# Down projection of a SwiGLU block: seven block products with stationary tokens, output by tokens

## The chip, the cores and the metric

The kernel runs on one core of one Trainium2 chip. The metric is the device time of one execution in microseconds (us). A profiled execution also leaves a trace: every instruction of the engines with its start and end, and the DMA transfers. In the trace PE is TensorE (matmul), DVE is VectorE, ACT is ScalarE, POOL is GpSimd, SP is the engine from whose queue the DMAs are issued.

## The reference

One layer of a residual block over 512 tokens with 2048 features: a mixing half (recurrent heads and attention heads), then a feed-forward half. Only the end of it is touched here:

```python
mod = silu(c) @ w_ada + b_ada                    # six rows of 2048: sh1, sc1, gt1, sh2, sc2, gt2
...
h2 = modulate(rms_norm(x, g_ffn), sh2, sc2)
gate, up = split(h2 @ w_up, 2)                   # w_up: 2048 x 11264, each half 5632 wide
x = x + gt2 * ((silu(gate) * up) @ w_down)       # w_down: 5632 x 2048, x: 512 x 2048
```

Everything is float32. Inside the kernel each factor of a large product is split into two parts that TensorE takes in its fp32r format, hi and lo, and a product is three matmuls: hi·hi, hi·lo, lo·hi.

## The kernel before

The kernel is traced by a planner: it records instructions in program order, finds the dependences, and orders each engine's instructions by a priority (program order, moved earlier by `tc.high_priority(offset=...)`) in a simulated run; on the chip each engine takes its own list in order. Buffers come from pools: a tile with a tag waits until one of the tag's buffers is free. The tags that matter here: "raw" and "raw2" (128x2048, two buffers each, weights as they come from memory), "whi" and "wlo" (128x1024, three each, the split halves of a weight chunk), and the pages of 128x512: "h" (32), "b" and "c" (16 each), "d" (4). PSUM has eight banks of 128x512: four in `acc`, three in `misc`, one in `rg`. `bank(i, f, name)` takes `acc` for an even i, the others for an odd one, so that neighbouring groups alternate.

Activations lie feature-major: a tile has 128 features on the partitions and 512 tokens along the free dimension. The stages are: input projections and recurrent part (`w1`, `yr`), eight head projections `h0` to `h7` with the attention of the head before as hooks between their steps, the output projection `wo`, and the feed-forward half:

- Two groups `up0`, `up1` (four 128-wide feature columns of w_up each, `fm_group`, 16 steps of 12 matmuls). During `up0`, at step 7 the sums and at step 9 the spread of the row norm `r1` are made on PE; from then on `make_t` forms the operands T of the fast products from h2 (`make_h2` also writes x1 to memory as `x1d`).
- Forty tiles `uf4` to `uf43` (line 1005): each makes one 128-wide tile of gate and of up by seven half-sized products instead of eight, with 168 matmuls of 256 columns. `fast_chunk` loads two weight chunks a tile (`uq_0r`, `uq_1r`, line 974), forms sums of their blocks on DVE (lines 982 to 986) and splits them: hi by ACT, lo by DVE (lines 210, 211). After a tile's matmuls, lines 1013 to 1020 combine the products and form silu(gate)·up. `spill_act` splits that into hi and lo and writes both to memory.
- The down projection `dn` in two parts of 24 and 20 feature tiles (`PARTS`), four groups of four output tiles each. The weights are stationary (128 features x 128 outputs), the activations move (512 tokens). All activation tiles of a part are read back first (`adh`, `adl`). The first part's sums go to memory as `dna`; the second part adds them, multiplies by gt2, adds x1 from memory and writes the output feature-major. The 16 rows of w_ada for gt2 (`ada_row`, `adr`) are multiplied on DVE during the first part.

The DMAs of all this are issued from the SP queue, in its order.

## Time and profile before

| | |
|---|---|
| runs | 2124.29, 2125.33, 2123.8 us; median 2124.29 |
| profiled execution | 2125.15 us, its span 2123.4 us |
| granted TensorE clock, mean | 0.995 |
| PE busy | 2088.6 us, 98% |
| DVE busy | 1518.3 us, 72% |
| ACT busy | 860.7 us, 41% |
| POOL busy | 33.9 us, 2% |
| moved by DMA | 405.98 MB, mean 191 GB/s |

The span is the time from the first to the last instruction in the trace; the execution's own time has a little around it. Busy time is the time in which an engine has an instruction running. A page of the profile further gives the chain of work that ended last (from the last instruction back to whatever released it, step by step), groups of instructions by line of the kernel, waits (who waited for whom), and windows: for a stretch of time the busy time of each engine, the clock that was granted to TensorE, the busy share of the 16 DMA engines and what they moved.

### The profile page before, as it was taken

To read this page: it belongs to the slowest core of one execution; us is meant where nothing else is said; L and a number is where in the kernel's file an instruction comes from. 1 tells how busy PE (TensorE), PEld (TensorE's weight loads), DVE (VectorE), ACT (ScalarE), POOL (GpSimd) and SP (SyncE) were. 2 spreads that over 40 slices of the span, in tenths; PEclk is the share of its full clock that TensorE was granted. 3 is DMA by queue.
4 is the path that set the end of the run, shared out by engine and by line. 5 is a ranking of instruction groups with operands and counts; after the bars stand their busy time and mean duration, and the time that the engine had idled before them with its cause. 6 is when DMAs were issued, how large, how long until landed. Compare 5 with 4: busy or idle time off the path is not lost.

```text
span 2123.4 us, 31896 instructions
## 1 busy us (share of the span) xinstructions
PE 2088.6 (98%) x12737; PEld 1898.2 (89%) x12737; DVE 1518.3 (72%) x2210; ACT 860.7 (41%) x1200; POOL 33.9 (2%) x37
## 2 busy tenths in 40 slices
PE   8999999999999998999999999999999999999999
PEld 6889898888788888999999999999999888888887
DVE  8999668886877789988888888888888362223332
ACT  4433447764532345444444444444444222221111
POOL 0000000000100000000000000000000000000000
PEclk9999999999999999999999999999999999999999
DMA  9989766667677522433333343343336995553442
GB/s 344 352 294 316 224 216 217 221 224 258 223 266 258 197 102 90 149 129 131 134 134 124 129 146 120 130 138 131 130 130 225 343 336 186 173 189 138 151 153 99
DMA packets 130710, 405.98 MB, mean 191 GB/s; under 512 B 14305, under 2 KB 19585, under 8 KB 118786
## 3 DMA queue, kind: packets, MB, share of 16 engines
q1 hardware_dynamic: 130562, 403.96, 54.7%
q8 instruction: 99, 1.62, 0.3%
q14 instruction: 49, 0.40, 0.1%
HBM read 361.15 MB, written 42.75 MB: 190 GB/s over the span
## 4 chain that ended last, share of the span: by engine, by line
PE 88%; DVE 7%; DMA 2%; issue 1%; ACT 1%; POOL 1%; SPq 0%; DVEq 0%; ACTq 0%
PE dn_0p L215 6%; PE dn_3p L215 6%; PE dn_2p L215 6%; PE dn_1p L215 6%; PE w1p L215 4%; PE yr1p L215 2%; PE up0p L215 2%; PE wo3p L215 2%; PE wo2p L215 2%; PE wo1p L215 2%; PE yr0p L215 2%; PE wo0p L215 2%; PE h3p L215 2%; PE h2p L215 2%; PE h7p L215 2%
## 5 line engine op out<-in xcount | busy, mean ns | idle before, releaser
L152 DVE SCALAR_TENSOR_TENSOR ada<-ada,c_b 128x1024 f32<-128x1024 f32 x96 | 116.0, 1218 | 28.0 <-DMA ada<-in_adaT 27.7
L211 DVE TENSOR_TENSOR uq_0al<-uq_0r,uq_0ah 128x1024 fp32r<-128x1024 f32 x40 | 49.0, 1224 | 61.5 <-ACT uq_0ah L210 61.5
L210 ACT ACTIVATE uq_0sh<-uq_0r 128x1024 fp32r<-128x1024 f32 x40 | 42.4, 1059 | 110.8 <-DVE uq_0r L983 110.8
L210 ACT ACTIVATE uq_1sh<-uq_1r 128x1024 fp32r<-128x1024 f32 x40 | 42.4, 1061 | 107.0 <-DVE uq_1r L983 102.4
L211 DVE TENSOR_TENSOR uq_0tl<-uq_0r,uq_0th 128x1024 fp32r<-128x1024 f32 x40 | 49.0, 1224 | 39.7 <-ACT uq_0th L210 39.7
L210 ACT ACTIVATE uq_0ah<-uq_0r 128x1024 fp32r<-128x1024 f32 x40 | 42.4, 1060 | 68.7 <-issue 5.1
L210 ACT ACTIVATE uq_1ah<-uq_1r 128x1024 fp32r<-128x1024 f32 x40 | 42.4, 1061 | 57.2 <-issue 57.0
L210 ACT ACTIVATE uq_0th<-uq_0r 128x1024 fp32r<-128x1024 f32 x40 | 42.4, 1060 | 48.5 <-DVE uq_0r L986 2.6
L211 DVE TENSOR_TENSOR uq_0sl<-uq_0r,uq_0sh 128x1024 fp32r<-128x1024 f32 x40 | 49.0, 1226 | 17.8 <-ACT uq_0sh L210 17.8
L215 PE MATMUL w1p<-hph,w1h 128*128 128x512 f32 x128 | 47.1, 396 | 5.1 <-ACT hph L356 5.1
L215 PE MATMUL w1p<-hpl,w1h 128*128 128x512 f32 x128 | 50.7, 396 | 0.0
L215 PE MATMUL w1p<-hph,w1l 128*128 128x512 f32 x128 | 50.4, 394 | 0.0
L211 DVE TENSOR_TENSOR uq_1tl<-uq_1r,uq_1th 128x1024 fp32r<-128x1024 f32 x40 | 49.0, 1225 | 0.9 <-ACT uq_1th L210 0.3
L982 DVE TENSOR_TENSOR uq_0r<-uq_0r 128x1024 f32<-128x1024 f32 x40 | 48.7, 1218 | 0.0
L211 DVE TENSOR_TENSOR uq_1al<-uq_1r,uq_1ah 128x1024 fp32r<-128x1024 f32 x40 | 48.6, 1215 | 0.0
L211 DVE TENSOR_TENSOR uq_1sl<-uq_1r,uq_1sh 128x1024 fp32r<-128x1024 f32 x40 | 48.6, 1215 | 0.0
L982 DVE TENSOR_TENSOR uq_1r<-uq_1r 128x1024 f32<-128x1024 f32 x40 | 48.5, 1213 | 0.0
L211 DVE TENSOR_TENSOR dn_1l<-dn_2r,dn_1h 128x1024 fp32r<-128x1024 f32 x11 | 13.5, 1226 | 42.8 <-ACT dn_1h L210 42.8
L211 DVE TENSOR_TENSOR dn_0l<-dn_2r,dn_0h 128x1024 fp32r<-128x1024 f32 x11 | 13.5, 1224 | 42.2 <-ACT dn_0h L210 42.2
L210 ACT ACTIVATE uq_1th<-uq_1r 128x1024 fp32r<-128x1024 f32 x40 | 42.5, 1063 | 0.6 <-PE uf43p L1005 0.3
L211 DVE TENSOR_TENSOR dn_1l<-dn_0r,dn_1h 128x1024 fp32r<-128x1024 f32 x11 | 13.5, 1225 | 39.4 <-ACT dn_1h L210 39.4
L211 DVE TENSOR_TENSOR dn_0l<-dn_0r,dn_0h 128x1024 fp32r<-128x1024 f32 x11 | 13.5, 1225 | 39.1 <-ACT dn_0h L210 39.0
(11827 smaller groups left out, 8139.3 us busy)
## 6 DMA issues: line engine op xcount, KB each, us to landing
ada<-in_adaT SPq DMA_DIRECT2D x128, 512.0 KB, 5.2
uq_1r<-in_wups SPq DMA_DIRECT2D x80, 512.0 KB, 4.1
uq_0r<-in_wups SPq DMA_DIRECT2D x80, 512.0 KB, 4.1
adf<-in_adaT SPq DMA_DIRECT2D x32, 512.0 KB, 5.7
adr<-in_adaT SPq DMA_DIRECT2D x16, 1024.0 KB, 6.9
actd<-ach SPq DMA_DIRECT2D x44, 256.0 KB, 2.0
actd<-acl SPq DMA_DIRECT2D x44, 256.0 KB, 2.0
dn_0r<-in_wdown SPq DMA_DIRECT2D x11, 1024.0 KB, 5.0
```

The costliest lines, as they stand in the source:

```text
L152: nc.vector.scalar_tensor_tensor(out=t, in0=t, scalar=1.0, in1=cs, op0=ALU.mult, op1=ALU.mult, accum_out=ac)
L210: nc.scalar.activation(R(hi[:, :n]), raw_ap, AF.Copy)
L211: tail_lo.append(nc.vector.tensor_sub(R(lo[:, :n]), raw_ap, hi[:, :n]).ins)
L215: nc.tensor.matmul(ps, lhsT=R(l), rhs=R(r), start=start, stop=stop)
L982: nc.vector.tensor_add(blocks[:, 0:3:2], blocks[:, 0:2], blocks[:, 2:3].broadcast_to([P, 2, 512]))
```

## The change

The down projection is written as one two-by-two block product by the Winograd form of Strassen's scheme: tokens are halved (2 x 256), outputs are halved (2 x 1024), and the features are divided into even and odd tiles. Seven products of 256 tokens x 2816 features x 1024 outputs take the place of eight. In each, the token block is stationary (128 features x 128 tokens) and 512 weight columns move. The products are done in four phases: P4 and P5, P1 and P7, P6, P2 and P3; a product holds four PSUM banks for its whole phase, and the results are combined on DVE after it.

The token operands are made after each pair of feature tiles (`keep_act`, four DVE operations of 256) and written to memory unsplit; the down stage reads them back and splits them. The weight operands are sums of blocks: those of two blocks are made on DVE from two loads (`dn_chunk`), the one of three blocks (S2) is made in memory during the up stage by a copy and accumulating DMAs issued from POOL (`sum2`). x1 is transposed on PE during `up0` and written by tokens (`x1_by_tokens`); gt2 is multiplied out during the up stage, in 64 pieces of 512 (`gt2_piece`), and later spread over the partitions (`gt2_spread`). The output is written by tokens. The last two chunks of P2 are kept, so that its four banks end one after the other.

```diff
-PARTS = [24, 20]
+X_STEPS = (2, 4, 6, 8)
+NQ = FT // 4
...
-    def ada_row(i):
-        t = bp.tile([P, D], F32, tag="raw2", name=f"adr{i}")
-        nc.sync.dma_start(out=t, in_=adaT[GT2 * KT + i])
-        nc.vector.scalar_tensor_tensor(out=t, in0=t, scalar=1.0, in1=c_b, op0=ALU.mult, op1=ALU.mult,
-                                       accum_out=ada_acc[GT2][:, 0, i:i + 1])
-        if i == KT - 1:
-            nc.vector.tensor_add(mods[GT2], ada_acc[GT2][:, 0, :], vec[:, V_BADA + GT2 * KT:V_BADA + (GT2 + 1) * KT])
+    gt2_acc = cp.tile([P, 4, KT], F32, name="gt2_acc")
+    gt2_src = {}
+
+    def gt2_load(n):
+        t = cp.tile([P, S], F32, name=f"gt2_{n}", tag="ssq", bufs=2)
+        nc.sync.dma_start(out=t, in_=adaT[GT2 * KT + n // 4, :, (n % 4) * S:(n % 4 + 1) * S])
+        gt2_src[n] = t
+
+    def gt2_piece(n):
+        if n == 0:
+            gt2_load(0)
+        if n < 4 * KT - 1:
+            gt2_load(n + 1)
+        t = gt2_src.pop(n)
+        r = n % 4
+        nc.vector.scalar_tensor_tensor(out=t, in0=t, scalar=1.0, in1=c_b[:, r * S:(r + 1) * S], op0=ALU.mult, op1=ALU.mult,
+                                       accum_out=gt2_acc[:, r, n // 4:n // 4 + 1])
+        if n == 4 * KT - 1:
+            m = mods[GT2]
+            nc.vector.tensor_add(m, gt2_acc[:, 0, :], vec[:, V_BADA + GT2 * KT:V_BADA + (GT2 + 1) * KT])
+            for r in range(1, 4):
+                nc.vector.tensor_add(m, m, gt2_acc[:, r, :])
...
-        x1d[kt] = drp.tile([P, S], F32, name=f"x1d{kt}")
-        nc.sync.dma_start(out=x1d[kt], in_=x1[kt])
         return t
+
+    def x1_by_tokens(a):
+        for t in range(NT):
+            pt = acc(f"x1p{a}_{t}")
+            for k in range(4):
+                nc.tensor.transpose(out=pt[:, k * P:(k + 1) * P], in_=x1[4 * a + k][:, t * P:(t + 1) * P], identity=ident)
+            w = page(f"x1w{a}_{t}", "d")
+            nc.scalar.activation(w, pt, AF.Copy)
+            x1t[t, a] = drp.tile([P, S], F32, name=f"x1t{a}_{t}")
+            nc.sync.dma_start(out=x1t[t, a], in_=w)
...
-    def spill_act(src, f):
-        hi, lo = page(f"ach{f}", "c"), page(f"acl{f}", "c")
-        nc.scalar.activation(R(hi), src, AF.Copy)
-        nc.vector.tensor_sub(R(lo), src, hi)
-        d = drp.tile([2, P, S], F32, name=f"actd{f}")
-        nc.sync.dma_start(out=d[0], in_=hi)
-        nc.sync.dma_start(out=d[1], in_=lo)
-        actd.append(d)
+    td = [[drp.tile([P, w, S], F32, name=f"td{ph}_{q}") for q in range(NQ)] for ph, w in enumerate((2, 2, 1, 2))]
+    s2d = [drp.tile([P, 2048], F32, name=f"s2d{q}") for q in range(NQ)]
+    even = []
+
+    def keep_act(o, f):
+        if f % 2 == 0:
+            even.append(o)
+            return
+        e = even.pop()
+        j = f // 2
+        q, ks = j // 2, slice((j % 2) * HS, (j % 2 + 1) * HS)
+        u, w = page(f"tu{j}", "c"), page(f"tw{j}", "c")
+        nc.vector.tensor_sub(u[:, :HS], e[:, HS:], e[:, :HS])
+        nc.vector.tensor_sub(w[:, :HS], e[:, HS:], o[:, HS:])
+        nc.vector.tensor_sub(w[:, HS:], u[:, :HS], o[:, HS:])
+        nc.vector.tensor_add(u[:, HS:], o[:, :HS], w[:, HS:])
+        nc.sync.dma_start(out=td[3][q][:, :, ks], in_=o.rearrange("p (a b) -> p a b", a=2))
+        nc.sync.dma_start(out=td[1][q][:, 0, ks], in_=e[:, :HS])
+        nc.sync.dma_start(out=td[0][q][:, :, ks], in_=u.rearrange("p (a b) -> p a b", a=2))
+        nc.sync.dma_start(out=td[1][q][:, 1, ks], in_=w[:, :HS])
+        nc.sync.dma_start(out=td[2][q][:, 0, ks], in_=w[:, HS:])
+
+    def sum2(q, n):
+        if n == 0:
+            nc.sync.dma_start(out=s2d[q], in_=wdn[0, q])
+        else:
+            for i in range(2):
+                cs = slice(i * 1024, (i + 1) * 1024)
+                nc.gpsimd.dma_start(out=s2d[q][:, cs], in_=wdn[n + 1, q, :, cs], accum_op=ALU.add)
...
-            spill_act(t, 2 * gi + f)
+            keep_act(t, 2 * gi + f)
...
+            for a in range(4):
+                add(hk, X_STEPS[a], lambda a=a: x1_by_tokens(a))
...
+            n = 2 * (f - 2 * STD) + c
+            if n < 4 * KT:
+                gt2_piece(n)
+            if n < 6 * NQ and n % 2 == 0:
+                sum2(n // 6, n // 2 % 3)
...
-        spill_act(g, f)
...
-            for n, (k, hi, lo) in enumerate(stream(src[:head // 4], list(range(head)), 512, f"dn{pi}_{g}")):
...
+        keep_act(g, f)
+
+    PHASES = (((4, 3, 1), (5, 2, 0)), ((1, 0, 0), (7, 2, 1)), ((6, -1, 0),), ((2, 1, 0), (3, -1, 1)))
+
+    def dn_load(tag, blk, q, nm):
+        pool = wp if tag == "raw" else bp
+        raw = pool.tile([P, 2048], F32, tag=tag, name=nm, bufs=RAW)
+        src = s2d[q] if blk < 0 else wdn[blk, q]
+        for i in range(2):
+            nc.sync.dma_start(out=raw[:, i * 1024:(i + 1) * 1024], in_=src[:, i * 1024:(i + 1) * 1024])
+        return raw
+
+    def dn_chunk(ph, q, hold=False):
+        prods = PHASES[ph]
+        out = {p: [] for p, _, _ in prods}
+        with tc.high_priority(offset=AHEAD):
+            raws, ts = [], []
+            for n, (p, blk, ix) in enumerate(prods):
+                nm = f"dq{p}_{q}"
+                raws.append(dn_load("raw2" if n or (len(prods) == 1 and q % 2) else "raw", blk, q, nm + "r"))
+                tl, th = page(nm + "tl", "h"), page(nm + "th", "h")
+                nc.sync.dma_start(out=tl, in_=td[ph][q][:, ix])
+                nc.scalar.activation(R(th), tl, AF.Copy)
+                nc.vector.tensor_sub(R(tl), tl, th)
+                ts.append((th, tl))
+            for n, (p, blk, ix) in enumerate(prods):
+                nm, raw = f"dq{p}_{q}", raws[n]
+                if n:
+                    nc.vector.tensor_add(raw, raw, raws[0])
+                for k in range(2):
+                    if hold and n == 0:
+                        w = []
+                        for i in range(2):
+                            src = raw[:, (2 * k + i) * S:(2 * k + i + 1) * S]
+                            hi, lo = page(f"{nm}h{k}{i}", "c"), page(f"{nm}l{k}{i}", "c")
+                            nc.scalar.activation(R(hi), src, AF.Copy)
+                            nc.vector.tensor_sub(R(lo), src, hi)
+                            w.append((hi, lo))
+                    else:
+                        hi, lo = wsplit(raw[:, k * 1024:(k + 1) * 1024], 1024, f"{nm}w{k}")
+                        w = [(hi[:, i * S:(i + 1) * S], lo[:, i * S:(i + 1) * S]) for i in range(2)]
+                    ks = slice(k * HS, (k + 1) * HS)
+                    out[p].append((w, ts[n][0][:, ks], ts[n][1][:, ks]))
+        return out
+
+    def dn_mm(ps, w, th, tl, tis, first, last):
+        for t in range(2):
+            c_ = slice(t * P, (t + 1) * P)
+            mine = [i for i in range(2) if (t, i) in tis]
+            for n, (st, part) in enumerate(((th, 0), (th, 1), (tl, 0))):
+                for i in mine:
+                    mm(ps[2 * t + i], st[:, c_], w[i][part], first and n == 0, last and n == 2)
+
+    ALL = [(t, i) for t in range(2) for i in range(2)]
+    gt2b = []
+
+    def gt2_spread():
+        pt = acc("gt2p")
+        nc.tensor.transpose(out=pt[:KT, :P], in_=mods[GT2], identity=ident)
+        row = page("gt2r", "d")
+        nc.scalar.activation(row[:KT, :P], pt[:KT, :P], AF.Copy)
+        gd = drp.tile([KT, P], F32, name="gt2d")
+        nc.sync.dma_start(out=gd, in_=row[:KT, :P])
+        gv = gd.rearrange("(a k) p -> a k p", k=4)
+        for a in range(4):
+            g = page(f"gt2b{a}", "h")
+            nc.sync.dma_start(out=g.rearrange("p (k m) -> p k m", k=4), in_=gv[a:a + 1].broadcast_to([P, 4, P]))
+            gt2b.append(g)
+
+    def finish(y, tt, a, nm, out=True):
+        xt = page(nm + "x", "d")
+        nc.sync.dma_start(out=xt, in_=x1t[tt, a])
+        nc.vector.tensor_mul(y, y, gt2b[a])
+        nc.vector.tensor_add(y, y, xt)
+        if out:
+            nc.sync.dma_start(out=outT[tt][:, a * S:(a + 1) * S], in_=y)
+
+    def last_out(ps, b, z, tt, nm):
+        i = b % 2
+        y = page(nm, "d")
+        nc.vector.tensor_mul(y, ps[b], gt2b[i])
+        nc.vector.tensor_add(y, y, z)
+        nc.sync.dma_start(out=outT[tt][:, i * S:(i + 1) * S], in_=y)
+
+    def copies(ps, nm):
+        r = []
+        with tc.high_priority(offset=EVAC):
+            for b in range(4):
+                r.append(page(f"{nm}{b}", "b"))
+                nc.scalar.activation(r[b], ps[b], AF.Copy)
+        return r
+
+    for ph, prods in enumerate(PHASES):
+        ps = {}
+        for n, (p, _, _) in enumerate(prods):
+            ps[p] = [bank((1 if ph < 3 else 2) + n, b, f"dn{p}p{b}") for b in range(4)]
+        held = []
+        for q in range(NQ):
+            hold = ph == 3 and q >= NQ - 2
+            out = dn_chunk(ph, q, hold)
+            if hold:
+                held += out.pop(prods[0][0])
+            for p, cells in out.items():
+                for k, cell in enumerate(cells):
+                    dn_mm(ps[p], *cell, ALL, q + k == 0, q == NQ - 1 and k == 1)
+            if ph == 2 and q == 2:
+                gt2_spread()
+        if ph == 0:
+            q4, q5 = copies(ps[4], "q4_"), copies(ps[5], "q5_")
+        elif ph == 1:
+            q1 = copies(ps[1], "q1_")
+            x_ = [page(f"dx{b}", "b") for b in range(4)]
+            with tc.high_priority(offset=EVAC):
+                for b in range(4):
+                    nc.vector.tensor_add(x_[b], ps[7][b], q5[b])
+                    nc.vector.tensor_add(q4[b], ps[7][b], q4[b])
+        elif ph == 2:
+            v = [page(f"dv{b}", "h") for b in range(4)]
+            with tc.high_priority(offset=EVAC):
+                for b in range(4):
+                    nc.vector.tensor_add(v[b], ps[6][b], q1[b])
+            for b, (t, i) in enumerate(ALL):
+                nc.vector.tensor_sub(q4[b], q4[b], v[b])
+                nc.vector.tensor_sub(x_[b], x_[b], v[b])
+                nc.vector.tensor_sub(q5[b], v[b], q5[b])
+                finish(q4[b], t, 2 + i, f"f21{b}")
+                finish(x_[b], 2 + t, 2 + i, f"f22{b}")
+                finish(q5[b], 2 + t, i, f"f12{b}", False)
+                finish(q1[b], t, i, f"f11{b}", False)
+        else:
+            for b, (t, i) in enumerate(ALL):
+                last_out(ps[3], b, q5[b], 2 + t, f"o12{b}")
+            for b, (t, i) in enumerate(ALL):
+                for k, cell in enumerate(held):
+                    dn_mm(ps[2], *cell, [(t, i)], False, k == len(held) - 1)
+                last_out(ps[2], b, q1[b], t, f"o11{b}")
...
+def _down(w):
+    import numpy as np
+    q = w.reshape(11, 2, 2, 128, 2, 1024).transpose(4, 2, 0, 3, 1, 5)
+    return np.ascontiguousarray(q).reshape(4, 11, 128, 2048)
...
-    args.append(nc.dram_tensor("out_T", (16, 128, 512), F32, kind="ExternalOutput").ap())
+    args.append(nc.dram_tensor("out_T", (4, 128, 2048), F32, kind="ExternalOutput").ap())
```

More of the change, by code (lines that the diff above doesn't have):

```diff
@@ L62, in block_kernel @@
 @with_exitstack
-def block_kernel(ctx, tc, xT, crow, adaT, vecs, bfr, w1, wyr, wqkv0, wqkv, wgate, wout, wup0, wups, wdown, outT):
+def block_kernel(ctx, tc, xT, crow, adaT, vecs, bfr, w1, wyr, wqkv0, wqkv, wgate, wout, wup0, wups, wdn, outT):
     nc = tc.nc
@@ L869, in block_kernel @@
     r1 = []
-    x1d = [None] * KT
+    x1t = {}
     T = {p: [None] * NP for p in range(1, 8)}
@@ L1020, in block_kernel @@
         nc.vector.tensor_mul(g, g, u)
-        spill_act(g, f)
-    dtags = ["b"] * 7 + ["h"] * 16 + ["b"] + ["c"] * 8 + ["b"] * 7 + ["h"] * 5
-    dn_a = [None] * KT
-    f0 = 0
-    for pi, part in enumerate(PARTS):
-        act = []
-        for f in range(f0, f0 + part):
-            hi, lo = page(f"adh{f}", dtags[f]), page(f"adl{f}", dtags[f])
-            nc.sync.dma_start(out=hi, in_=actd[f][0])
-            nc.sync.dma_start(out=lo, in_=actd[f][1])
-            act.append((hi, lo))
-        last = pi == len(PARTS) - 1
-        for g in range(4):
-            src = wdown[g, f0 // 4:(f0 + part) // 4]
-            ps = [bank(g + 1, f, f"dn{pi}_{g}p{f}") for f in range(4)]
-            hk = {}
-            if not last:
-                for i, n in enumerate((4, 9, 14, 19)):
-                    add(hk, n, lambda i=4 * g + i: ada_row(i))
-            ends = last and g == 3
-            head = part - 4 if ends else part
-            for n, (k, hi, lo) in enumerate(stream(src[:head // 4], list(range(head)), 512, f"dn{pi}_{g}")):
-                for f in range(4):
-                    fs = slice(f * P, (f + 1) * P)
-                    mm(ps[f], hi[:, fs], act[k][0], n == 0, False)
-                    mm(ps[f], hi[:, fs], act[k][1], False, False)
-                    mm(ps[f], lo[:, fs], act[k][0], False, n == part - 1)
-                for fn in hk.get(n, ()):
-                    fn()
-            ws = list(stream(src[head // 4:], list(range(4)), 512, f"dt{pi}_{g}")) if ends else []
-            for f in range(4):
-                kt = g * 4 + f
-                fs = slice(f * P, (f + 1) * P)
-                for k, hi, lo in ws:
-                    ah, al = act[head + k]
-                    mm(ps[f], hi[:, fs], ah, False, False)
-                    mm(ps[f], hi[:, fs], al, False, False)
-                    mm(ps[f], lo[:, fs], ah, False, k == 3)
-                if not last:
-                    t = page(f"dnt{kt}", "d")
-                    nc.scalar.activation(t, ps[f], AF.Copy)
-                    dn_a[kt] = drp.tile([P, S], F32, name=f"dna{kt}")
-                    nc.sync.dma_start(out=dn_a[kt], in_=t)
-                else:
-                    y = page(f"dny{kt}", "d")
-                    nc.sync.dma_start(out=y, in_=dn_a[kt])
-                    xt = reload(x1d[kt], f"x1l{kt}")
-                    nc.vector.tensor_add(y, ps[f], y)
-                    nc.vector.scalar_tensor_tensor(out=y, in0=y, scalar=mods[GT2][:, kt:kt + 1], in1=xt,
-                                                   op0=ALU.mult, op1=ALU.add)
-                    nc.sync.dma_start(out=outT[kt], in_=y)
-        f0 += part
@@ L1118 @@
         "wups": _quads(w_up),
-        "wdown": np.stack([_pieces(w_down[:, i * 512:(i + 1) * 512]) for i in range(4)]),
+        "wdn": _down(w_down),
     }
@@ L1131 @@
     o = r.results[0]["out_T"]
-    return np.ascontiguousarray(o.reshape(2048, 512).T).reshape(1, 512, 2048)
+    return np.ascontiguousarray(o).reshape(1, 512, 2048)
```

1 line of the change is left out of this document (removed).

## The prediction

> **What bounds the kernel now.** I read the page's engine totals first, then the chain that ended last.
>
> ```profile
> span 2123.4 us, 31896 instructions
> PE 2088.6 (98%) x12737; PEld 1898.2 (89%) x12737; DVE 1518.3 (72%) x2210; ACT 860.7 (41%) x1200; POOL 33.9 (2%) x37
> PE 88%; DVE 7%; DMA 2%; issue 1%; ACT 1%; POOL 1%; SPq 0%; DVEq 0%; ACTq 0%
> ```
>
> TensorE (PE) is busy 98% of the span and is itself 88% of the chain. The same chain in order of time (start, duration, what) shows the last stages as unbroken matmuls:
>
> ```profile
> 466.43 10.41 PE h7p L215 x60
> 476.84 0.87 PE qkt L504 x8
> ...
> 1620.10 20.16 PE uf43p L1005 x168
> 1640.26 65.31 PE dn_0p L215 x288
> ...
> 2064.61 54.41 PE dn_3p L215 x240
> ```
>
> Each piece begins where the one before it ended, so nothing but the number of matmuls sets this time. 65.31/288 = 0.2268 us for each matmul with 512 moving columns. The windows view (stretch: length, busy time of PE, weight load, DVE, ACT, POOL, granted clock, DMA share, GB/s) says the same of whole stages:
>
> ```profile
> 753.00:763.06 10.06, 10.06 (x54) 8.60 (x53) 1.45 (x3) 2.11 (x2) 2.16 (x2) 1.00 0.29 104
> 763.06:833.00 69.94, 64.44 (x294) 53.91 (x294) 66.20 (x113) 41.72 (x63) 0.00 (x0) 0.96 0.23 80
> 820.00:833.00 13.00, 7.50 (x39) 6.63 (x39) 10.78 (x18) 7.11 (x11) 0.00 (x0) 0.79 0.14 42
> 1217.06:1237.22 20.16, 20.16 (x170) 20.16 (x169) 16.80 (x21) 9.05 (x12) 0.00 (x0) 1.00 0.39 132
> 1640.26:1705.57 65.31, 65.31 (x289) 54.08 (x289) 28.23 (x28) 15.91 (x19) 0.00 (x0) 1.00 0.90 331
> 1640.26:2119.02 478.76, 478.75 (x2112) 396.19 (x2111) 160.28 (x152) 101.27 (x105) 0.00 (x0) 1.00 0.55 199
> 2119.02:2123.40 4.38, 0.00 (x0) 0.00 (x0) 1.45 (x2) 0.00 (x0) 0.00 (x0) 0.76 0.24 89
> ```
>
> The down projection is 478.76 us long, PE never waits in it, and VectorE (DVE) is used for a third of it: 160.28 us. The up stage (one feature tile in 20.16 us) is also PE-bound, but there DVE works 16.80 of 20.16 us. Only at 763 to 833, the start of the up stage, is DVE (66.20 of 69.94) the limit.
>
> **The down products.** 44 feature tiles x 16 output tiles x 3 = 2112 matmuls become 7 products x 22 pairs x 4 banks x 3 = 1848, all 512 columns wide. 478.76/2112 = 0.22669 us, times the 264 removed: **−59.84 us**. Tokens are now stationary and weights move. The trace has that order already in the head projections, with 384 columns: 10.41/60 = 0.1735 us. From the feature-stationary stages, 0.1200 at 256 (20.16/168) and 0.2267 at 512, a straight line puts 384 at 0.1733. So the order costs nothing. The weight load takes 396.19/2111 = 0.188 us, below 0.2267, so it stays covered.
>
> The Trainium skill ("TensorE: Matmul & The Clock Gate", section on 56 against 53.3 ns) gives N/2.4 GHz plus about 2.5 ns from start to start, 215.7 ns for 512 columns. The rows here have 226.7 ns for fp32 data. With the page's figure the gain would be 56.9 us and the sum about 3 us higher; I go by the rows.
>
> **x1 by tokens.** 64 transposes of 128x128 enter the first up group at its steps 2, 4, 6 and 8. Eight cost 0.87 us in the row of the head transposes, so 64 cost **+7.0 us** on PE. They stand ahead of the sums and the spread of the row norms, which release the DVE-bound stretch 763 to 833. Here are the release and the wait in which that stretch ends (waits: total, times, longest):
>
> ```profile
> 762.16 0.89 PE rstd_1b L285 x8
> PE bup_p L942 <- DVE bu_acc L916: 5.5, 1, 5.5
> ```
>
> Before the release DVE is nearly idle (1.45 of 10.06 us), so nothing can be made up: the whole 7.0 us shifts. Ends: 5.2 (the last of four steps hidden) to 9 (a bank or page wait added). The 16 copies by ACT (0.6 us each) fit, ACT being busy 2.11 of 10.06. The 16 writes of x1t replace 16 of x1d on the SP queue.
>
> **Handing the activation on.** These rows give the costs used here and below:
>
> ```profile
> 1224.08 0.68 DVE L983 TENSOR_TENSOR uq_1r<-uq_1r 128x512 f32<-128x512 f32 x1
> 1224.69 0.41 DVE L1018 TENSOR_TENSOR uu<-uf22p,uw 128x256 f32<-128x256 f32 x1
> 1226.22 1.21 DVE L211 TENSOR_TENSOR uq_1sl<-uq_1r,uq_1sh 128x1024 fp32r<-128x1024 f32 x1
> 1231.14 0.28 PE L1005 MATMUL uf23p<-td4h,uq_1sh 128*128 128x256 f32 x1
> 1641.27 1.22 DVE L211 TENSOR_TENSOR dn_0l<-dn_0r,dn_0h 128x1024 fp32r<-128x1024 f32 x1 [1.66 <-ACT dn_0h L210]
> 1642.41 0.68 DVE L1014 TENSOR_TENSOR ug<-uf43p,uw 128x512 f32<-128x512 f32 x1
> 1644.53 0.41 DVE L1018 TENSOR_TENSOR uu<-uf43p,uw 128x256 f32<-128x256 f32 x1
> 1691.29 2.28 DVE L168 SCALAR_TENSOR_TENSOR adr<-adr,c_b 128x2048 f32<-128x2048 f32 x1
> 1693.50 0.08 DVE L168 DVE_READ_ACCUMULATOR adr<-adr,c_b 128x1 f32 x1
> ```
>
> For each pair of feature tiles, two subtractions of 512 (2 x 0.68) and two ACT copies go, four operations of 256 (4 x 0.41) come: +0.14 us of DVE a tile. The gt2 rows move from the down stage, where DVE had room, into the up stage, as two pieces of 512 a tile: 2 x (0.68 + 0.08) = 1.52. DVE goes from 16.80 to about 18.5 of 20.16 us, 92%. What covers it is the lead of the weight split: uq_1sl ends at 1227.43 and PE first touches its pair at 1231.14, 3.7 us later. 1.7 us of extra work inside a 3.7 us lead costs **0** (0 to 5 over the stage). If the cover goes, each late microsecond counts once per tile, 40 times.
>
> Two transfers stand behind waits now. The SP queue waits long for raw buffers, and the gt2 loads and the five writes of a pair queue there:
>
> ```profile
> SPq L974 <- DVE uq_0tl L211: 338.4, 38, 9.5
> actd<-ach SPq DMA_DIRECT2D x44, 256.0 KB, 2.0
> dn_0r<-in_wdown SPq DMA_DIRECT2D x11, 1024.0 KB, 5.0
> 187.79 1.65 POOL ss L264
> ```
>
> A gt2 load is issued one piece (10.1 us) ahead. At worst it stands 9.5 us behind a raw load and takes about 2 us to land: 1.4 us late, inside the lead. The output tiles of the second up group now hold "d" pages until a write has landed (2.0 us, where the ACT and DVE readers released them before), and the first fast chunks need those pages: **+2 us** (0 to 8, the upper end being four such landings in a row). The additions for S2 run on the POOL queue, which had no work there, and are needed only some 250 us later: 0 unless they hold DVE (rival below).
>
> **DVE in the down stage.** A chunk of two products is 48 matmuls, 10.88 us. DVE does four splits of 1024 (1.14 from start to start, 1641.27 to 1642.41), two of 512 (0.61) and one addition of 2048 (nearest row 2.21 from start to start): 8.0 us, 73%. Before, it had 33%; the up stage runs at 83% without a PE wait, through the same three-deep split buffers, so phases 0 to 2 cost 0. In phase 3 come 44 finishing operations of 512 as well: 26.8 us beside 88 us, in 120 us. The splits have priority, so I take **+3** (0 to 26.8: all of it uncovered).
>
> **Boundaries.** The products P5 reuse the banks of feature tile 43 about 5.4 us (24 matmuls) after it ends. In the trace its last read ends at 1644.94, 4.7 us after 1640.26; with a busy DVE, tile 22's last read ended at 1225.10, 8.1 us after its matmuls. So 0 to 2.4, **+1.2**. Later boundaries copy four banks inside the 5.4 us of another product: 0. The gt2 transpose is 0.1. The end keeps its form (two DVE operations and one 256 KB store after the last matmul, 4.38 us): 0.
>
> **Transfers of the down stage.** 77 weight chunks of 1.05 MB and 77 token chunks of 0.26 MB are 101 MB in 419 us, 241 GB/s; the first stretch of the old stage moved 331 GB/s with PE never waiting. A raw buffer comes free about two chunks (21.8 us) before PE needs it again, and a megabyte lands in 5.0. Cost 0.
>
> **Sum:** 2123.4 − 59.84 + 7.0 + 0 + 2 + 3 + 1.2 + 0.1 = 2076.9 span. The profiled execution took 2125.15, 1.75 over its span, giving 2078.6; the median of the runs, 2124.29, is 0.86 below that execution. Predicted: **2078**.
>
> **Rivals.** (a) DVE becomes the bound of the down stage: finishing work pushes splits behind it, or addition and split run in a strict chain. With the finish uncovered the time is 2078 + 23.8 = 2102; half of it, 2090. For: 115 us of DVE work in phase 3's 120. Against: the up stage at 83%.
>
> (b) Fewer matmuls, no gain: transfers bind. At the old stage's mean of 199 GB/s the 101 MB take 507 us against 419, so 2166, slower. This decides below 101/(419 + 46) = 217 GB/s. Against: 331 GB/s above. For: two buffers a tag and half-sized loads, which no row shows at this rate.
>
> (c) The other side through the up stage: POOL's accumulating DMAs (44 issues in 33 tiles, 1.33 a tile) hold DVE's path to memory while they are issued. No row has their price; the longest POOL operation here takes 1.65 us. At that, 2.2 us a tile makes DVE 20.7 of 20.16: 0.5 x 33 = 18 us, 2096. The kernel gets slower than before from 46/33 = 1.4 us of wait a tile, that is at (20.16 + 1.4 − 18.5)/1.33 = 2.3 us an issue; at 3 us it would be 2078 + 77 = 2155. The Trainium skill ("SBUF — State Buffer", Who interferes with whom) says that a two-input VectorE operation contends with GpSimd work that reads SBUF, and not with work that only writes it. Descriptors are written, so that rule speaks against this rival; no trace here has such a DMA.
>
> **How the numbers follow.** Forecast, 2069 to 2084: 0.58. Rival (a), 2084 to 2104: 0.22. Rival (b): 0.05 slower, 0.03 within 0.2% of before (the bound of what can be told from no change), 0.03 between. Rival (c): 0.05 faster still, 0.03 slower. Below 2069: 0.01, as the sum with only the transposes' lower end is 2123.4 − 59.84 + 5.2 + 0.9 = 2069.7. So faster 0.89, same 0.03, slower 0.08; from 2069 to 2100 I leave out about 0.16.
>
> **What the changed profile would show.** PE in the down stage: 1848 matmuls at 0.2267, 419 us, and waits of PE there only in single microseconds; 64 transposes and a release of the row norms about 7 us later; DVE at 90 to 93% in a middle tile with the tile still 20.16 us; DVE near 80% in the pair phases and highest in phase 3. I am wrong if a middle tile takes more than 20.16 us (DVE or POOL), if PE waits for DMA on raw chunks, or if splits of the products come after PE has asked for them.

## The result, and the profile after

| | before | after |
|---|---|---|
| median | 2124.05 us (4 runs) | 2218.85 us (4 runs, 2215.34 to 2223.3) |
| profiled execution, span | 2125.15, 2123.4 us | 2223.3, 2221.6 us |
| granted TensorE clock, mean | 0.995 | 0.964 |

The ratio is 1.0447 with an interval from 1.0423 to 1.0471: slower by 95 us where 46 us less was predicted. From the page of the changed kernel, its totals and the shares of the chain that ended last:

```profile
span 2221.6 us, 32358 instructions
PE 2064.6 (93%) x12538; PEld 1873.0 (84%) x12538; DVE 1742.0 (78%) x2573; ACT 951.7 (43%) x1316; POOL 68.3 (3%) x81
PE 72%; DMA 12%; DVE 11%; issue 3%; POOL 1%; ACT 1%; SPq 1%; DVEq 0%; POOLq 0%; ACTq 0%
```

PE does 199 instructions less (the 264 matmuls saved, 64 transposes added, one of gt2) and yet is down from 98% to 93%; transfers, 2% of the chain before, are 12%. The windows say where (length, then busy time of PE, weight load, DVE, ACT, POOL, granted clock, DMA share, GB/s). The changed kernel:

```profile
249.00:480.00 231.00, 133.09 (x637) 120.97 (x635) 82.97 (x157) 67.50 (x127) 40.47 (x48) 0.75 0.99 249
290.00:330.00 40.00, 2.87 (x17) 2.54 (x15) 1.23 (x2) 2.54 (x4) 8.04 (x10) 0.60 1.01 235
850.50:957.60 107.10, 100.46 (x494) 84.57 (x492) 92.53 (x163) 59.33 (x91) 2.11 (x2) 0.98 0.44 152
957.60:1765.40 807.80, 807.80 (x6710) 807.80 (x6710) 699.40 (x963) 340.12 (x405) 0.00 (x0) 1.00 0.43 141
1765.40:1887.00 121.60, 120.58 (x530) 98.84 (x529) 96.69 (x90) 63.76 (x77) 0.00 (x0) 1.00 0.72 248
1887.00:2006.50 119.50, 119.50 (x529) 98.94 (x528) 87.41 (x74) 59.14 (x69) 0.00 (x0) 1.00 0.68 233
2006.50:2081.00 74.50, 60.88 (x258) 49.85 (x257) 37.35 (x38) 27.53 (x31) 0.00 (x0) 0.89 0.61 208
2081.00:2217.20 136.20, 125.92 (x538) 101.05 (x536) 123.41 (x142) 56.44 (x69) 0.00 (x0) 0.97 0.70 235
```

The first two of these stretches in the kernel before:

```profile
249.00:480.00 231.00, 223.85 (x1224) 204.63 (x1223) 183.99 (x337) 151.84 (x273) 14.27 (x10) 0.99 0.64 213
290.00:330.00 40.00, 40.00 (x220) 36.33 (x218) 28.11 (x55) 24.23 (x46) 2.73 (x2) 1.00 0.61 193
```

At 249 to 480 us the kernel does the head projections, which the diff does not touch. There PE works 133 of 231 us instead of 224, and for 40 us hardly at all, with the DMA engines full. The DMA view of this stretch, changed kernel (queues: packets, MB, share of 16 engines; issues: count, KB each, median us to landing):

```profile
q0 software_dynamic: 6336, 23.07, 58.0%
q1 hardware_dynamic: 8333, 34.39, 40.5%
s2d<-in_wdn POOLq DMA_DIRECT2D x44, 512.0 KB, 12.1
ada<-in_adaT SPq DMA_DIRECT2D x20, 512.0 KB, 16.3
h4r<-in_wqkv SPq DMA_DIRECT2D x4, 768.0 KB, 15.4
```

and before:

```profile
q1 hardware_dynamic: 16794, 48.90, 64.1%
ada<-in_adaT SPq DMA_DIRECT2D x46, 512.0 KB, 4.4
h4r<-in_wqkv SPq DMA_DIRECT2D x4, 768.0 KB, 4.8
```

All 44 accumulating DMAs of S2, written into the up stage, stand here (shortest, median and longest issue in ns, then the first and the last start):

```profile
L970 POOL DMA_DIRECT2D s2d<-in_wdn x44: 802/823/1216, 257.4 to 470.5; - x44
```

They need only the S2 copies, which need nothing that the kernel makes, so the planner was free to put them early: the first starts at 257 us, 700 us ahead of the fast tiles (from 957.5) in whose loop they were written. They move 23.07 MB in 58% of the engines' time; SP's own 34.39 MB take 40.5%. The loads of the head stage then land two to seven times later, the two shown 3.7 and 3.2 times.

The balance, from the first matmuls of each stage in the two traces (the output projection's, before and after):

```profile
L215 PE MATMUL wo0p<-mx8h,wo_0h x4: 389/389/389, 553.0 to 555.0; 128*128 128x512 f32 x4
L231 PE MATMUL wo0p<-mx8h,wo_0h x4: 389/389/389, 669.5 to 671.5; 128*128 128x512 f32 x4
```

The output projection starts at 669.5 instead of 553.0 (**+116.5**); the first up tiles at 957.5 instead of 832.5 (**+8.5** more); forty tiles at 20.16 as before; the four phases of the down stage 121.6, 119.5, 74.5 and 136.2 us, against 1848 x 0.2267 = 418.9 in all (**+32.9**); the saved matmuls **−59.8**. Together +98.1, and the span grew by 98.2.

### The profile page after: what moved, and what is told of

The parts are those of the page before. It is cut to its first block, busy times and chain, and to the rows that moved or that the text cites. A ratio compares the mean times of both kernels' runs of the same rounds, so it can differ in the third digit from the quotient of the medians.

```text
span 2221.6 us, 32358 instructions
## 1 busy us (share of the span) xinstructions
PE 2064.6 (93%) x12538; PEld 1873.0 (84%) x12538; DVE 1742.0 (78%) x2573; ACT 951.7 (43%) x1316; POOL 68.3 (3%) x81
## 3 DMA queue, kind: packets, MB, share of 16 engines
q0 software_dynamic: 6336, 23.07, 6.0%
## 4 chain that ended last, share of the span: by engine, by line
PE 72%; DMA 12%; DVE 11%; issue 3%; POOL 1%; ACT 1%; SPq 1%; DVEq 0%; POOLq 0%; ACTq 0%
DMA s2d<-in_wdn 5%; PE w1p L231 4%; PE dn6p L231 3%; PE dn7p L231 3%; PE dn1p L231 3%; PE dn5p L231 3%; DMA ada<-in_adaT 2%; PE dn4p L231 2%; PE yr1p L231 2%; PE up0p L231 2%; PE wo3p L231 2%; PE wo2p L231 2%; PE wo1p L231 2%; PE yr0p L231 2%; PE wo0p L231 2%
## 5 line engine op out<-in xcount | busy, mean ns | idle before, releaser
L227 DVE TENSOR_TENSOR uq_0sl<-uq_0r,uq_0sh 128x1024 fp32r<-128x1024 f32 x40 | 49.0, 1225 | 16.3 <-ACT uq_0sh L226 16.3
L181 DVE SCALAR_TENSOR_TENSOR gt<-gt,c_b 128x512 f32<-128x512 f32 x64 | 43.8, 686 | 18.9 <-DMA gt<-in_adaT 18.6
L513 DVE TENSOR_TENSOR qk<-qk,ss 128x512 f32<-128x512 f32 x16 | 10.7, 689 | 48.5 <-POOL ss L280 48.5
L541 PE MATMUL s<-qkT,qkT 128*128 128x128 f32 (+3 forms) x64 | 25.7, 505 | 22.1 <-DVE nm L546 17.1
L520 PE MATMUL qkt<-ident,qk 128*128 128x128 f32 x64 | 10.1, 310 | 38.4 <-DVE qk L513 38.4
```

Of the source, the lines that this page charges most:

```text
L181: nc.vector.scalar_tensor_tensor(out=t, in0=t, scalar=1.0, in1=c_b[:, r * S:(r + 1) * S], op0=ALU.mult, op1=ALU.mult, accum_out=gt2_acc[:, ...
L227: tail_lo.append(nc.vector.tensor_sub(R(lo[:, :n]), raw_ap, hi[:, :n]).ins)
L513: nc.vector.tensor_tensor(z, z, ss[:, 4 * a:4 * a + 4].unsqueeze(2).broadcast_to([P, NT, P]), ALU.mult)
L520: nc.tensor.transpose(out=pt[:, t * P:(t + 1) * P], in_=z[:, t, :], identity=ident)
L541: nc.tensor.matmul(ps[:, :n], lhsT=qT[:, bs], rhs=kT[:, :n], start=True, stop=False)
```

## The experiments

Each ratio is to the kernel before, run on the same chip. "After" is the changed kernel.

**e6: the old kernel with the S2 transfers alone.** The kernel before gets `sum2` (11 copies from SP, 44 accumulating DMAs from POOL) and its call in the loop over the fast tiles:

```diff
+            n = 2 * (f - 2 * STD) + c
+            if n < 66 and n % 2 == 0:
+                sum2(n // 6, n // 2 % 3)
```

> The old kernel with the S2 copies and accumulating DMAs added alone (from the old w_down array, result unused), traced at the same places of the up stage. Queue and traffic theory: the planner pulls them to the head stage as it did in the changed kernel, and the old kernel becomes about 116 us slower, 2240 us (2220 to 2260). Rival, the rest of the change stretches the head stage: 2124, no change.

Measured 2237.24 us, ratio 1.0519 [1.0498, 1.054], +109. The transfers alone, whose result nothing reads, cost more than the whole change lost. **e3** is the counterpart, the changed kernel with `sum2` reduced to its copy, so that an S2 buffer holds one block and not the sum of three:

> The changed kernel with the 44 accumulating transfers left out, and nothing else edited: the S2 buffers then hold one block where they should hold the sum of three, so the output is another. Theory (these transfers alone make the mixing stage's 116 us; the gt2 chain's 14 us, the last phase's 16 us, the 7 transposes and a few us stay): 2219 - 113 = 2106 (2100 to 2113), with the output projection starting near 553. Rival (a part of the mixing stage's loss is of other new instructions, the order of the engines' queues above all): 2120 or more.

2110.5 us, ratio 0.9925 [0.9911, 0.994]. Its windows in the head stage:

```profile
249.00:480.00 231.00, 224.45 (x1215) 204.43 (x1214) 183.59 (x337) 150.69 (x271) 14.39 (x10) 0.99 0.75 262
290.00:330.00 40.00, 40.00 (x220) 36.33 (x219) 28.68 (x55) 25.13 (x47) 2.85 (x2) 1.00 0.80 289
```

The stage is whole again with eleven plain 1 MB copies still in it, and the output projection starts at 553.5. The accumulating transfers cost 108 us, more than the whole loss of 95.

**e10: e6 with plain copies** (`accum_op=ALU.add` left out, so the S2 buffers hold no sums; same bytes, same queue).

> The old kernel with the S2 transfers alone, as in the run at 2237 us, but the 44 POOL DMAs copy instead of accumulating (the result is not used): same bytes written, same waits and same places in POOL's queue. Theory that the accumulating form itself is dear (23.07 MB in 0.58 of 231 us, 172 GB/s, where the other queue's bytes move at 367): the engine time halves and 2237 falls to 2150 to 2190 us. POOL queue theory: the norms still stand behind the same 44 issues and waits, 2225 to 2240. Rival, any 34 MB more in the head stage: 2225 to 2240 as well.

2189.58 us, ratio 1.0304 [1.0285, 1.0323]: 48 us less than e6. The DMA view at 249 to 480 us, first e6, then e10:

```profile
q0 software_dynamic: 6336, 23.07, 55.8%
```

```profile
q0 software_dynamic: 6336, 23.07, 29.1%
```

The same 6336 packets and 23.07 MB take half the engine time without the addition. The rest, 64 us, is what the plain transfers cost when they are thrown together into a stage that used 64% of the DMA engines, with what they hold up in POOL's queue.

**e2: is it the order of POOL's queue?** In after, the head norms (`ss`, POOL) stand behind up to 44 DMA issues, and before 24 of them POOL waits for an earlier transfer:

```profile
POOL s2d L970 <- DMA s2d<-in_wdn: 137.7, 24, 14.0
```

e2 makes the norms on DVE and ACT. A second edit, not shown, queues the S2 copies behind a load of the first head, which keeps them in the head stage.

```diff
-            rms_rstd(ss, ss, HEAD_DIM)
+            nc.vector.tensor_scalar(out=ss, in0=ss, scalar1=1.0 / HEAD_DIM, scalar2=EPS, op0=ALU.mult, op1=ALU.add)
+            nc.scalar.activation(ss, ss, AF.Sqrt)
+            nc.vector.reciprocal(ss, ss)
```

> S2 stays in the head stage, its first copy pinned behind the cb load of head 0, but the head norms leave POOL: mean and epsilon on DVE, square root on ACT, reciprocal on DVE. Queue theory: the waits for ss go, and most of the 116 us come back, less up to 20 us for the square root's table loads on ACT: 2105 to 2150 us. Traffic theory: the loads and so the head stage stay as slow, 2200 to 2235 us.

2204.8 us, ratio 1.0366 [1.0345, 1.0387]: 14 us less than after and inside the range of the traffic theory; the output projection starts at 652.4, still 99 us late. The square root brings 16 more table loads of 1.28 us on ACT, which may hide up to 20 us of what the queue was worth. Even so the queue is the smaller part; in the stretch from 249 to 480 us the DMA engines are full in e2 too (share 1.01).

**e1: the S2 transfers where they were written.** `issue_after` only orders an instruction behind another in its queue; here behind the last POOL operation of the row norm, and behind the last write of x1t on SP:

```diff
+                with tc.issue_after(pool_last[-1]):
+                    nc.gpsimd.dma_start(out=s2d[q][:, cs], in_=wdn[n + 1, q, :, cs], accum_op=ALU.add)
```

> The sums for S2 (the copies on SP and the accumulating DMAs on POOL) are queued behind the last POOL operation and the last x1t write of the first up group; nothing else changes. Queue theory (the norms of heads 3 to 8 stand behind the accumulating DMAs in POOL's in-order queue): the head and mixing stages return to their length in the old kernel, wo0 starts at about 553 us instead of 669.6, and the time is 2219 - 116 = 2103 us (2095 to 2112). Traffic theory (the accumulating DMAs take the DMA engines from the head stage's loads): the same here, since the traffic goes too. Rival, gt2 pieces or x1 by tokens at fault: no change, 2219.

2176.12 us, ratio 1.0242 [1.0215, 1.0268], 73 us above both theories. The head stage is whole (output projection from 552.0), but the bunch now starves the up stage. A window and the DMA queues (769 to 960 us) of e1:

```profile
830.00:870.00 40.00, 19.48 (x72) 15.56 (x73) 24.15 (x39) 13.88 (x21) 8.39 (x11) 0.67 1.05 241
q0 software_dynamic: 6192, 22.56, 63.4%
q1 hardware_dynamic: 6657, 27.14, 40.4%
```

So the place was not the fault alone: nothing but their own order spaces the transfers out, and 22.56 MB of them in 191 us fill the engines in this stage too.

**e7: one step a tile.** A one-element POOL copy of the tile's product makes each step wait for its tile; the plain copies stand behind the tile's last activation write.

```diff
+        tick = small(1, f"tick{f}")
+        pool_last.append(nc.gpsimd.tensor_copy(out=tick, in_=g[:, :1]).ins)
```

> Each S2 step is tied to its place: the accumulating DMAs behind a one-element POOL copy that reads the product of the tile before, the SP copies behind the last write of the pair before. So four accumulating DMAs and one copy fall on every three tiles of the up stage. Saturation theory (an accumulating DMA takes the 16 engines for about 3 us, 0.58 of 231 us for 44 of them, and bunched they starve every other load): paced, they fill 0.28 of three tiles beside 0.43, nothing starves, tiles stay at 20.16 us, and the time is 2219 - 116 = 2103 us (2096 to 2112). Rival, a POOL DMA holds DVE or the loads wherever it stands: tiles with S2 lengthen, the 33 tiles together by 40 us or more, 2140 to 2180.

2142.11 us, ratio 1.0079 [1.0065, 1.0093]: 77 us less than after, 39 short of expectation. What was left stood in two places. One is the phase P6, where PE waits once, 13.6 us in after. After's waits in the down stage, and SP's queue in order of time (start, duration):

```profile
PE dn6p L231 <- ACT dq_3th L1093: 13.6, 1, 13.6
PE dn2p L231 <- ACT dq_0th L1093: 6.6, 1, 6.6
```

```profile
2022.61 0.80 SPq L1080 DMA_DIRECT2D dq_7r<-s2d  x2
2024.22 0.32 SPq L1133 DMA_DIRECT2D gt2d<-gt2r  x1
2024.60 0.42 SPq L1142 DMA_DIRECT2D f210x<-x1t  x1
...
2028.07 1.74 SPq L1137 DMA_DIRECT2D gt2b<-gt2d  x4
2029.86 0.42 SPq L1092 DMA_DIRECT2D dq_3tl<-td  x1
```

The weights of chunk 7 are issued, but the tokens of chunk 3 stand behind gt2's way to memory and back (`gt2_spread`). **e5** (on e1) and **e8** (on e7) move its transpose and write into the up stage, behind the last gt2 piece, and leave only the four `gt2b` loads in P6 (`gt2_load_b`).

```diff
             if n < 4 * KT:
                 gt2_piece(n)
+            if n == 4 * KT + 1:
+                gt2_spread()
...
             if ph == 2 and q == 2:
-                gt2_spread()
+                gt2_load_b()
```

> As the run with S2 late, and besides the transpose of gt2 and its write to memory move from the third chunk of P6 into the up stage, two tiles behind the last gt2 piece; only its four broadcast loads stay at P6. Queue theory for SP (the token loads of P6's chunks 3 to 7 stand behind the gt2 chain in SP's queue): the wait of 13.6 us in P6 goes, about 2089 us (2083 to 2096), and P6 takes 60 us. Rival, the token loads wait for pages: no difference to the run with S2 late, about 2103.

> Paced S2, and the gt2 transpose and its write in the up stage. The two theories about SP's queue as before: the 13 us wait in P6 goes, 2103 - 13 = 2090 us (2083 to 2098), faster than the old kernel by 1.2 to 2%; if the chip's S2 cost is in every place the same, 2130 or more.

e5: 2162.59 us, 13.5 less than e1. e8: 2127.23 us (11 runs), 14.9 less than e7, and level with the kernel before (ratio 1.0009). In e8's chain P6 is one piece:

```profile
1928.88 57.13 PE dn6p L231 x252
```

**Why e8 is not at 2090.** Eight tiles, uf5 to uf12, took 193 us instead of 161. Two windows of e8, and pieces of its chain:

```profile
866.90:1060.00 193.10, 169.63 (x1342) 168.20 (x1342) 152.70 (x245) 65.80 (x81) 13.98 (x20) 0.94 0.66 188
1060.10:1221.40 161.30, 161.30 (x1347) 161.30 (x1346) 136.42 (x178) 68.04 (x82) 20.18 (x18) 1.00 0.64 185
884.03 10.14 DMA gt<-in_adaT
911.04 14.18 DMA gt<-in_adaT
...
1028.21 12.14 DMA gt<-in_adaT
```

The planner also set the gt2 pieces early, up to tile 12. Those of the chain, beside accumulating transfers, land after 10 to 14 us, and DVE, which takes its list in order, waits for them with the weight splits behind. **e11** spread the loads of the pieces over tiles 4 to 35:

```diff
+        with tc.issue_after(sp_last[-1]):
-        nc.sync.dma_start(out=t, in_=adaT[GT2 * KT + n // 4, :, (n % 4) * S:(n % 4 + 1) * S])
+            nc.sync.dma_start(out=t, in_=adaT[GT2 * KT + n // 4, :, (n % 4) * S:(n % 4 + 1) * S])
```

> The kernel of e8 with the 64 loads of the gt2 pieces paced as the accumulating transfers are: each load is queued behind the last activation write of the tile before it, so that they spread over tiles 4 to 35 in place of tiles 4 to 12. In e8 the eight tiles uf5 to uf12 took 193.2 us where 161.3 is usual (+31.9), and the chain there runs through DMA gt<-in_adaT pieces of 10 to 14 us. Theory (two bunches meet: gt2 pieces and accumulating transfers together keep the weights waiting): all tiles back to 20.16, 2127 - 30 = 2097 (2090 to 2106). Rival 1 (the accumulating transfers slow those tiles by themselves, gt2 only shows it): the loss stays, 2120 or more. Rival 2 (the later gt2 additions now fill DVE in every tile, which then sets the tile): each tile of uf4 to uf36 above 20.5, 2110 to 2135.

2126.79 us, ratio 0.9997 [0.9987, 1.0007]: nothing gained, so the theory of two bunches falls. The loss spread along with the pieces: as long as there were pieces the tiles took 21.0 to 21.3 us on average (single ones 20.1 to 26.8), with DVE waiting for them (e11, ten tiles from 1200 us; total, times, longest):

```profile
DVE gt L183 <- DMA gt<-in_adaT: 23.3, 7, 6.7
```

The time also lies in the range of e11's second rival, a full DVE, but DVE is busy only 168 of these 200 us. Nor is it the pieces alone: in after, 34 of the 64 stand in tiles 4 to 11 with no accumulating transfer beside them, DVE is busy 97% of the time there, and PE still runs unbroken (all pieces, then the window of these eight tiles):

```profile
L181 DVE SCALAR_TENSOR_TENSOR gt<-gt,c_b x64: 675/684/694, 736.8 to 1117.8; 128x512 f32<-128x512 f32 x64
957.60:1119.00 161.40, 161.40 (x1324) 161.40 (x1324) 156.86 (x257) 68.53 (x82) 0.00 (x0) 0.98 0.57 186
```

What is left is pieces beside accumulating transfers. **e13** leaves the pieces early and starts S2 seven tiles later:

```diff
-            if n < 6 * NQ and n % 2 == 0:
-                sum2(n // 6, n // 2 % 3)
+            z = n - 14
+            if 0 <= z < 6 * NQ and z % 2 == 0:
+                sum2(z // 6, z // 2 % 3)
```

> The kernel of e8 with the S2 transfers seven tiles later (tiles 11 to 43 in place of 4 to 36), so that the gt2 pieces, which the planner sets up to about tile 12, are nearly past when the accumulating transfers begin. In e11 spreading the gt2 pieces under the accumulating transfers gave tiles of 21.0 to 21.3 us up to uf36 and 20.17 behind it, DVE waiting 23.3 us in ten tiles for gt<-in_adaT; in e8 tiles with accumulating transfers but no gt2 pieces took 20.16. Theory (a late gt2 piece at the head of DVE's order is what the accumulating transfers cost; alone they cost the tiles nothing): of the 31.9 us some 28 go, 2127 - 28 = 2099 (2092 to 2108). Rival (the loss is that of the accumulating transfers wherever they stand, at about 1 us a tile): 2120 to 2130.

2107.83 us, ratio 0.9913 [0.99, 0.9926]. In its chain the tiles run unbroken under the accumulating transfers:

```profile
1008.27 20.16 PE uf12p L1065 x168
...
1593.01 20.16 PE uf41p L1065 x168
```

S2 alone costs the tiles nothing there. Twenty tiles of e13 with S2 issues on POOL, then twenty of after without any, show that DVE is not slowed either (337.77 and 337.78 us):

```profile
1200.00:1603.20 403.20, 403.20 (x3363) 403.19 (x3362) 337.77 (x441) 168.37 (x202) 48.44 (x49) 1.00 0.64 183
1200.00:1603.20 403.20, 403.20 (x3362) 403.20 (x3362) 337.78 (x441) 168.42 (x200) 0.00 (x0) 1.00 0.39 128
```

But the last S2 transfers meet the first down weights (dq_0r landed in 11.7 us; the first phase, P4 and P5, took 128.9). **e15** uses n − 10, **e17** the range of tiles 11 to 41 (`n == 14 + z * 15 // 8` for the 33 steps z).

> The kernel of e13 with the S2 transfers at tiles 9 to 41 in place of 11 to 43. In e13 the first phase of the down stage took 128.9 us (1658.4 to 1787.3) where 119.7 is the matmuls' own and 123.2 was seen in e11; PE waited 6.9 us for dq_0w1l, and its weights, issued at 1625.9 beside the last accumulating transfers, took 11.7 us to land. Theory (the last accumulating transfers delay the first down weights): 6 of them go, 2108 - 6 = 2102 (2098 to 2105). Rival 1 (the loads of that stretch are late for another reason, token loads in a burst): within 2 us of 2108. Rival 2 (the earlier start meets the last gt2 pieces again): 2110 or more.

> The kernel of e13 with the 33 S2 steps spread over tiles 11 to 41 (a step every 15/16 of a tile) in place of 11 to 43. e13 lost no time in tiles 6 to 42 (20.16 each) but 6.9 us at the start of the first down phase; e15 lost nothing there but 10.4 us in tiles 11 and 12, to gt2 pieces. Theory (both losses are meetings, and neither is left): 2105.5 - 10 = 2096 (2093 to 2100). Rival (the denser transfers cost the tiles some time of their own): 2101 to 2108.

e15: 2105.52 us; the first phase took 122.6, but tiles 11 and 12 lost 10.2 to the last pieces (1.6 and 8.6). e17: **2101.33 us** (2099.21 to 2104.94), ratio **0.9879 [0.9862, 0.9895]**, one microsecond above its expected range and inside its rival's (denser transfers cost the tiles time). The trace speaks for the theory: the last pieces still met the first steps in tile 12 (26.9 us), and behind it the tiles are back at 20.16. By its median it is the fastest version, 1.2% below the kernel before.

**The last phase.** P2 and P3 take 136.2 us in after with the wait ahead of them, against 120 for their matmuls. **e9** leaves out of e8 the 32 finishing operations (product with gt2, addition of x1; the four quarters are then unfinished), transfers kept.

```diff
-        nc.vector.tensor_mul(y, y, gt2b[a])
-        nc.vector.tensor_add(y, y, xt)
```

> As the paced kernel with gt2 early, but the 32 finishing multiplications and additions of the combined products are left out (the transfers of x1 and the stores stay), so DVE has 20 us less to do in the last two phases; the output lacks gt2 and x1 in part. DVE theory for phase 3 (16 us over 119.7): about 10 to 16 us less, 2074 to 2080. Rival, the order of SP's queue and the token loads set phase 3: at most 3 us less, 2087 or more.

2127.37 us against e8's 2127.23: no gain, where the theory on DVE expected 2074 to 2080. In the profiles the middle of the phase is better, e8 first, then e9:

```profile
2004.00:2070.00 66.00, 61.86 (x265) 50.19 (x264) 59.53 (x66) 29.60 (x34) 0.00 (x0) 0.97 0.81 277
```

```profile
2004.00:2070.00 66.00, 65.99 (x292) 54.27 (x291) 52.10 (x47) 31.93 (x37) 0.00 (x0) 1.00 0.75 253
```

but the medians do not show it, and e8's profiled execution was 5 us above its median. **e12** (on e11) and **e16** (on e15) take the loads of x1 and the stores of finished quarters off SP's queue:

```diff
-        nc.sync.dma_start(out=xt, in_=x1t[tt, a])
+        nc.gpsimd.dma_start(out=xt, in_=x1t[tt, a])
...
-            nc.sync.dma_start(out=outT[tt][:, a * S:(a + 1) * S], in_=y)
+            nc.gpsimd.dma_start(out=outT[tt][:, a * S:(a + 1) * S], in_=y)
```

and order the down weights behind the token loads, e12 in all phases, e16 in the last alone.

> The kernel of e11 with the queue order of the last phase mended: the loads of x1 and the stores of the finished quarters go out from POOL's queue in place of SP's, and each load of down weights is queued behind the token load before it. In e8 the last phase took 137.1 us instead of 119.7 and SP waited there 16.5 us and 3.4 us with finished quarters (out_T<-q, out_T<-dx) at the head of its queue, and the first token load stood behind the weights of chunk 2. Theory (SP's order makes the late loads of the last phase): 12 of the 17.4 us go, e11 - 12, about 2085 (2079 to 2091). Rival 1 (DVE's finishing arithmetic sets the phase; leaving it out in e9 took 6 us off the phase in the profile): within 4 us of e11. Rival 2 (transfers issued by POOL are dear, as the accumulating ones were): e11 or slower.

> The kernel of e15 with SP's queue mended in the last phase only: the loads of x1 and the eight stores of finished quarters are issued by POOL, and the down weights from chunk 2 on stand behind the token loads of the chunk before. e12 had a like edit in all phases, which held up the first phase by 15 us; from the start of the third phase to the end it was 3.2 us shorter than e11. Theory (SP's order makes a third or more of the last phase's loss): e15 - 6, about 2096 (-3 to -9). Rival (DVE's load sets the last phase, as POOL's additions, which slowed DVE's operations from 1.15 to 1.77 us and cost 9 us, speak for): within 3 us of e15.

e12: 2141.02 us, as its order made the first weights wait for the last up tile (first phase 16 us later); from P6 to the last matmul it was 3.2 shorter than e11. e16: 2104.71 against e15's 2105.52, within the spread. In e16's trace the first matmul of P2 comes 61.7 us after that of P6, not 66.6, but from there to the last matmul it takes 131.3 us, not 127.1: what the order gains at the boundary is lost behind it. SP's order alone does not set the phase. **e14** (on e13) gives POOL the 16 additions of x1, and the eight stores of finished quarters as in e16.

```diff
-        nc.vector.tensor_add(y, y, xt)
+        nc.gpsimd.tensor_add(y, y, xt)
```

> The kernel of e13 with the 16 additions of x1 in the last phase done by POOL in place of DVE, and their stores issued by POOL. In e11 DVE was busy 122 of the 140 us from 1990, and in e9, without the 32 finishing operations, the phase was 6 us shorter. Theory (DVE's load, near full in the last phase, is a part of its 17 us, and POOL can take 9.6 us of it): e13 - 5, about 2094 (-3 to -8 against e13). Rival 1 (POOL's additions hold DVE off while they run, or are so slow that the pages they keep come free too late): no better than e13, or slower by up to 10. Rival 2 (the raw buffers' round alone sets the phase): within 1.5 us of e13.

2117.31 us against 2107.83: 9 slower. A DVE split on 128x1024 of the last phase in e13 (count, busy us, mean ns, idle before), then e14's timeline, where POOL's additions overlap it:

```profile
L227 DVE TENSOR_TENSOR dq_3w0l<-dq_3r,dq_3w0h 128x1024 fp32r<-128x1024 f32 x2 | 2.4, 1220 | 0.0
```

```profile
2015.81 1.67 POOL L1158 TENSOR_TENSOR q<-q,f212x 128x512 f32<-128x512 f32 x1 [10.10 <-DVE q L1157]
2016.25 2.32 DVE L227 TENSOR_TENSOR dq_3w0l<-dq_3r,dq_3w0h 128x1024 fp32r<-128x1024 f32 x1
2026.92 1.21 DVE L227 TENSOR_TENSOR dq_3w0l<-dq_3r,dq_3w0h 128x1024 fp32r<-128x1024 f32 x1
```

Beside an addition of POOL the split takes 2.32 us instead of 1.21. So DVE is busy longer in e14's last phase (122.6 us against 115.9) with 16 operations fewer. The stores from POOL cost nothing in e16, so they are not the likely cause. DVE made slower costs time, but DVE relieved (e9) gains none that the medians show. How the phase's 16 us divide between DVE, the boundary (6.6 us for the first tokens) and the two-deep raw buffers is not settled.

## Why the prediction was wrong

- **The step that failed** is the sentence on S2: "The additions for S2 run on the POOL queue, which had no work there, and are needed only some 250 us later: 0 unless they hold DVE (rival below)." It took the place of the call for the place in time, and it asked what the transfers wait for, not what waits for the DMA engines beside them. Measured: 108 us in the changed kernel (e3), 109 in the old one (e6). The kernel's description had the fact at hand that a planner sets the order; these transfers depended on nothing that would have kept them in the up stage. None of the three signs of being wrong looked at the head stage.
- **Rival (c)**, POOL's issues holding DVE, named the same transfers but another mechanism. e13 shows 30 tiles at 20.16 us with such issues in them, and DVE as busy as without them: they do not hold DVE. That agrees with the Trainium skill's "SBUF — State Buffer" (Who interferes with whom). POOL work that reads SBUF is the other half of that rule, and e14 shows it (1.21 to 2.32 us).
- **The transfers of the down stage, put at 0,** held for the bytes: 248 GB/s in P4 and P5, and 233 in P1 and P7 with PE unbroken. Rival (b), which needed a rate under 217, falls. But the path of gt2 through SP's queue, costed at 0.1 us as a transpose, made P6 wait 13.6. What stands in the queue behind a moved step was asked of the up stage and not of P6.
- **The finish, +3 (0 to 26.8)**, measured +16.4 with its boundary, inside the range. Rival (a) was right about the place and DVE's load (123 us, forecast 115 in 120), but the runs don't show DVE to be the cause: without the finishing operations (e9) the time was the same.
- **Right:** the cadence (1848 at 0.2267; 252 in 57.13 us), the 64 transposes (the release of the row norms comes 35.2 us after the first matmul of `up0`, not 28.2: +7.0, as forecast), and the boundary of P5 (121.6 for 119.7, forecast +1.2; by its own rows, 8.1 less 5.4, the upper end of that term is 2.7 and not 2.4, which changes nothing). From that release to the first fast tile it is 1.4 us more (forecast 2), but gt2 pieces stand there too, so the hand-on is not measured by itself. The cadence is that of the rows; by an estimate from the figure of the Trainium skill ("TensorE: Matmul & The Clock Gate") 252 matmuls would have taken 54.4 us, and the measurement decides.
- **The tile at 20.16** was right too, under another load than forecast. No gt2 piece came to a middle tile, and DVE is at 84% in the twenty tiles of after shown under e13. The planner had set the pieces ahead of tile 12, where they brought DVE to 97% (forecast 92), and the lead of the weight splits covered even that.
- With the failed steps mended (e17), the median is 2101.33 against the 2078 forecast, so 1.2% below the kernel before where 2.2% was forecast. What is left is the last phase (some 12 over its term), 7 in tile 12 and single microseconds elsewhere.

## What to carry to other kernels

A transfer that depends on nothing has no fixed place in a program that a planner orders: pin it to a work item, so that both its place and its pace are set, and look in the trace where it landed. Cost a bulk transfer by its share of DMA engine time and by what else loads in that stretch, not by when its result is needed. A step that makes something small go to memory and back holds up every load behind it in its queue; do it where that queue has slack.
